# Evictions of the down result and transposes of the activations one place later in a mixture-of-experts stage

## The chip, the cores and the metric

The kernel runs on one core of a Trainium2 chip. The metric is the device time of one execution in microseconds (us). The core has a matmul engine (TensorE, PE in the profile; PEld are its weight loads), a vector engine (VectorE, DVE), a scalar engine (ScalarE, ACT), GpSimd (POOL, hardly used here) and SyncE (SP), which issues the transfers of the weights. Each engine runs its own list of instructions in order.

## The reference

Three transformer blocks on 256 tokens of width 1024 follow each other. The change is in the last step of the third, a mixture of 32 experts with four experts per token:

```python
def block_ffn(args):
    xb, e = args
    act = clamped_swiglu(xb @ w1[e] + b1[e])
    return act @ w2[e] + b2[e]
...
contrib = gate_sorted[:, None].astype(h.dtype) * y_buf[dest]
return jnp.zeros((T, D), h.dtype).at[sorted_tok].add(contrib)
```

A gate weighs each expert's result for each of its tokens, and the results are added. All inputs are float32.

## The kernel before

The method `moe` takes the experts in the order of their number of tokens, one per round `r`, 0 to 31. The first four (`BIGS`) have 128 rows for tokens, the others 64. A round has two parts. `up(r)` (L1840) multiplies the tokens of expert `r` with its up weights, 8 units of 1 MB each, 128x2048. `down(q, r)` (L1857) multiplies the activations of an earlier expert (from round 6 on `q = r - 2`) with its down weights, 4 units. So a round needs 12 MB.

A unit comes by a transfer into one of seven buffers (`raw` five times, `rawm`, `rawx`). Then `split` (L507) makes two halves of it: ACT writes the high half `whi` (L509), DVE subtracts it and writes the low half `wlo` (L510). There are three buffers for each half. PE multiplies with `whi`, then with `wlo`. For experts from 4 on, unit 1 of each part is not split; PE reads its raw buffer (`plain`), and the buffer is free when PE is through. All other buffers are free when DVE's subtraction is through.

All other work is put between the units by hand. `at(r, slot, f)` enters a step at one of 12 places of a round, and `run` calls the steps of a place: places 0 to 7 stand behind the first matmuls of the units of `up`, 8 to 11 in `down`. Each engine's list is exactly in this written order (`manual_schedule`). A step at place k stands on ACT and DVE behind the split of unit k and before that of unit k+1, and on PE between unit k's matmuls with `whi` and those with `wlo`.

The steps that matter here:

- `weigh(z, n)` (L1939), n = 0 and 1, evicts one half of the down result of expert `z = r - 3` from PSUM, times the gates: ACT writes `yh` (L1945), DVE writes `yl` (L1946). It waits for the down matmuls at the end of the round before.
- `activate(t)`, `silu(t)`, `gated(t)` work in even rounds on the up results of experts `r - 2` and `r - 1`, which share a tile: DVE clamps (L1878, L1879) at place 0, ACT takes silu (L1882) at place 1, DVE multiplies (L1886) at place 2.
- `turn(t)` (L1917) transposes these activations on PE, 8 matmuls of 128x128 into `atp` (L1923). `atp` and the down result `p2` share one PSUM buffer. Its `out(n)` (L1934, L1935) evicts them at places 6 and 7.
- `combine` (L1958) adds `yh` and `yl` of two experts to the output: matmuls `cbp` at places 4 to 7 of even rounds, an addition on DVE one place later.
- `take` and `fold` (L1898, L1911) at places 10 and 11 copy and add the up result. `gather` (`gp`, L1770, L1776) brings the tokens of four experts together, once per four rounds, in the down part of rounds 6, 10, ..., 26 and the up part of the odd rounds behind them.

After round 31 a tail works off experts 30 and 31; it doesn't use the places.

Of the kernel before, what the change touches and what calls it, by code (L numbers as in the profile page):

```python
# [434 lines left out]
class Net:  # L435
# [1202 lines left out]
    def moe(s, x, nm, ctx):  # L1638
# [114 lines left out]
        def gather(r, n):  # L1753


            G = mp.tile([128, 2, n, 128], F32R, name="G", tag="G", bufs=1)
            slots, w = ("iota", 128) if n == 2 else ("twice", SMALLS)
            for t in range(2):
                for a in range(n):
                    nc.vector.tensor_scalar(G[:, t, a], k_(slots), pos[:, t, r + a:r + a + 1], None,  # L1760
                                            op0=ALU.is_equal)
            xg = [mp.tile([128, 8, 2, 128], F32R, name="gx", tag="gx", bufs=3) for _ in range(2)]
            for a in range(n):
                X[r + a] = (xg[a][:, :, 0], xg[a][:, :, 1]) if n == 2 else xg[a // 2][:, :, a % 2]

            def chunk(k):
                p = aux("gp", (128, n, 2, w))
                for i, src in enumerate((hh, hl)):
                    for t in range(2):
                        mm(p[:, :, i], src[:, t, k * 128:(k + 1) * 128], G[:, t, :, 0:w], start=t == 0,  # L1770
                           stop=t == 1)

                def out():
                    for a in range(2):
                        q = p[:, a] if n == 2 else p[:, 2 * a:2 * a + 2].rearrange("p a b c -> p a (b c)")
                        nc.scalar.activation(xg[a][:, k], q, AF.Copy)  # L1776
                return out
            return [lambda k=k: chunk(k) for k in range(8)] + [lambda a=a: scatter(r + a, G[:, :, a])
                                                               for a in range(n)]
# [46 lines left out]
        def at(r, slot, *fs):  # L1826

            steps.setdefault((r + slot // 12, slot % 12), []).extend(fs)
# [5 lines left out]
        def pair_of(step, r, slot, behind=2):  # L1834

            at(r, slot, lambda: at(r, slot + behind, step()))
# [44 lines left out]
        def silu(r):  # L1881
            nc.scalar.activation(A[r][:, 0:1024], A[r][:, 0:1024], AF.Silu, scale=ALPHA)  # L1882

        def gated(r):
            b = A[r]
            nc.vector.scalar_tensor_tensor(b[:, 1024:2048], b[:, 1024:2048], 1.0, b[:, 0:1024], op0=ALU.add,  # L1886
                                           op1=ALU.mult)

        def take(r):

            p = P[r]
            if big(r) or r % 2 == 0:
                A[r] = mp.tile([128, 2048], F32, name="ml", tag="ml", bufs=1)
            if big(r):
                return bound(A[r], p[:, 0:1024], p[:, 1024:2048])
            own, other = halves(r)
            for ns in (slice(0, 1024), slice(1024, 2048)):
                nc.scalar.activation(A[r - r % 2][own, ns], p[other, ns], AF.Copy)  # L1898
# [5 lines left out]
        def fold(r, n):  # L1904

            if big(r):
                return
            own, _ = halves(r)
            ns = slice(n * 1024, n * 1024 + 1024)
            b = A[r - r % 2][own, ns]  # L1910
            nc.vector.tensor_add(b, b, P[r][own, ns])  # L1911

        def activate(r):
            if not big(r):
                bound(A[r], A[r][:, 0:1024], A[r][:, 1024:2048])

        def turn(r):  # L1917

            b = A[r]
            p = s.bank("atp", (128, 8, 128), "p2", 1)  # L1920
            t = mp.tile([128, 8, 2, 128], F32R, name="tp", tag="tp", bufs=1)
            for k in range(8):
                nc.tensor.transpose(p[:, k], b[:, 1024 + k * 128:1152 + k * 128], ident)  # L1923
            if big(r):
                hi, lo = A[r] = t[:, :, 0], t[:, :, 1]
            else:
                t5 = t.rearrange("p k a (b c) -> p k a b c", b=2)
                hi, lo = t5[:, :, :, 0], t5[:, :, :, 1]
                p = p.rearrange("p k (a c) -> p k a c", a=2)
                A[r], A[r + 1] = t[:, :, 0], t[:, :, 1]  # L1930

            def out(n):
                ks = slice(4 * n, 4 * n + 4)
                nc.scalar.activation(hi[:, ks], p[:, ks], AF.Copy, scale=1.0 / ALPHA)  # L1934
                nc.vector.scalar_tensor_tensor(lo[:, ks], p[:, ks], 1.0 / ALPHA, hi[:, ks].bitcast(F32),  # L1935
                                               op0=ALU.mult, op1=ALU.subtract)
            return out

        def weigh(r, n):  # L1939

            if n == 0:
                Y[r] = [mp.tile([128, 1024], F32R, name=a, tag=a, bufs=2) for a in ("yh", "yl")]
            yh, yl = Y[r]
            ns = slice(n * 512, n * 512 + 512)
            nc.scalar.activation(yh[:, ns], P[r][:, ns], AF.Copy, scale=GS[r])  # L1945
            nc.vector.scalar_tensor_tensor(yl[:, ns], P[r][:, ns], GS[r], yh[:, ns].bitcast(F32),  # L1946
                                           op0=ALU.mult, op1=ALU.subtract)
# [10 lines left out]
        def combine(r, c2):  # L1958

            p = aux("cbp", (128, 2, 256))  # L1960
            for c in range(2):
                back(p[:, c], 2 * c2 + c, (r, r + 1))
            o = acc[:, 2 * c2:2 * c2 + 2]
            return lambda: nc.vector.tensor_add(o, o, p)  # L1964
# [30 lines left out]
        for r in range(32):  # L1995
            q = r - 1 if r < BIGS else r - 2

            d = {0: (), 1: (), BIGS: (BIGS - 2,), BIGS + 1: (), BIGS + 2: (BIGS - 1,)}.get(
                r, (r - 2,) if r < BIGS else (r - 3,))
            for z in d:  # L2000
                at(r, 1, lambda z=z: weigh(z, 0))
                at(r, 2, lambda z=z: weigh(z, 1))
                if z % 2:
                    for c2 in range(4):
                        pair_of(lambda z=z, c2=c2: combine(z - 1, c2), r, 4 + c2, 1)
            t = r - 1 if r <= BIGS else r - 2 if r % 2 == 0 else -1
            if t >= 0:
                at(r, 0, lambda t=t: activate(t))
                at(r, 1, lambda t=t: silu(t))
                at(r, 2, lambda t=t: gated(t))  # L2010

                def turned(t=t, r=r):
                    out = turn(t)
                    at(r, 6, lambda: out(0))
                    at(r, 7, lambda: out(1))
                at(r, 3, turned)
            if r != 0:
                at(r, 9 if r == BIGS else 10, lambda r=r: take(r))
                at(r, 9 if r == BIGS else 10, lambda r=r: fold(r, 0))
                at(r, 9 if r == BIGS else 11, lambda r=r: fold(r, 1))  # L2020
            if r == 3 or r % 4 == 2 and BIGS < r < 30:
                g = r + 1 if r == 3 else r + 2
                spots = [(3, k) for k in range(12)] if r == 3 else (
                    [(r, 8 + k) for k in range(4)] + [(r + 1, k) for k in range(8)])

                def begin(g=g, spots=spots):
                    for f, (rr, k) in zip(gather(g, 4), spots):
                        if (rr, k) == spots[0]:
                            at(rr, k + 2, f())
                        else:  # L2030
                            pair_of(f, rr, k)
                at(*spots[0], begin)
# [238 lines left out]
```

## Time and profile before

| | |
|---|---|
| median of 3 runs | 2798.61 us (2796.19 to 2800.68) |
| the profiled execution | 2793.71 us, span 2791.9 us |
| busy in the span: PE, PEld | 2717.9 us (97%), 2364.8 us (85%) |
| busy in the span: DVE, ACT | 2245.2 us (80%), 1683.1 us (60%) |
| transfers over the span | 728.97 MB, 261 GB/s |
| transfers in fortieths 28 to 39 of the span | 384 to 413 GB/s |

The third block's experts fill the stretch from about 1680 us to the end. The span counts from the first instruction to the last; the time is the whole execution. In the timelines a row is one instruction, or several alike in a row (x8), with its start, its length, the names of what it writes and reads, and in brackets the idle time of the engine just before it and what ended that. `p` stands for the PSUM tiles of the up and the down product: `p<-whi,gx` is an up matmul, `p<-whi,tp` a down matmul.

### The profile page before, as it was taken

What the parts mean: (1) busy time and instruction counts of PE and PEld (TensorE: products, weight loads), DVE (VectorE), ACT (ScalarE), POOL (GpSimd) and SP (SyncE); (2) the same over time, 40 slices, a digit from 0 to 9 for tenths busy, and PEclk for the clock granted to TensorE, in tenths of its full rate; (3) what the DMA queues carried; (4) which work ended last, traced back from release to release, by engine and by line L of the source; (5) the groups of instructions that cost most, each with busy time, mean ns of one, the idle gap of its engine ahead of it and who ended that gap; (6) DMA issues with size and microseconds to landing.
All of it is one profiled execution on the core that took longest, in us unless ns stands there. A gap on an engine that the chain in (4) does not pass through costs nothing. (4 is left out here: it accounts for less than half of the span.)

```text
span 2791.9 us, 45884 instructions
## 1 busy us (share of the span) xinstructions
PE 2717.9 (97%) x17764; PEld 2364.8 (85%) x17764; DVE 2245.2 (80%) x3537; ACT 1683.1 (60%) x2658; POOL 3.3 (0%) x10
## 2 busy tenths in 40 slices
PE   9999999999999999999999998999999999999996
PEld 9999999999988999889999866877776767676764
DVE  7776777787776778888777754989999899999995
ACT  6554454464544545664467645777777777777773
POOL 0000000000000000000000000000000000000000
PEclk9999999999999999999999998999999999999998
DMA  7664466666653666437632333989999999999994
GB/s 290 229 227 166 173 221 240 244 224 242 227 182 122 236 243 225 150 139 256 234 142 96 111 118 120 359 306 384 395 405 395 398 402 389 405 387 400 388 413 161
DMA packets 102433, 728.97 MB, mean 261 GB/s; under 512 B 11384, under 2 KB 12920, under 8 KB 14528
## 3 DMA queue, kind: packets, MB, share of 16 engines
q1 hardware_dynamic: 99648, 719.64, 67.0%
q10 hardware_dynamic: 2560, 6.32, 0.7%
q8 instruction: 143, 2.34, 0.3%
q14 instruction: 82, 0.67, 0.1%
HBM read 723.80 MB, written 2.11 MB: 260 GB/s over the span
## 5 line engine op out<-in xcount | busy, mean ns | idle before, releaser
L510 DVE TENSOR_TENSOR wlo<-raw,whi 128x512 fp32r<-128x512 f32 (+1 forms) x1238 | 1178.7, 990 | 199.8 <-ACT whi L509 195.7
L509 ACT ACTIVATE whi<-raw 128x512 fp32r<-128x512 f32 (+1 forms) x1238 | 1006.6, 867 | 518.3 <-issue 283.1
L515 PE MATMUL gu<-xh,whi 128*128 128x256 f32 (+1 forms) x1760 | 499.7, 284 | 2.1 <-ACT whi L509 2.1
L517 PE MATMUL gu<-xh,wlo 128*128 128x256 f32 (+1 forms) x1760 | 497.6, 283 | 0.7 <-DVE wlo L510 0.7
L516 PE MATMUL gu<-xl,whi 128*128 128x256 f32 (+1 forms) x1760 | 498.1, 283 | 0.0
L515 PEld LDWEIGHTS gu<-xh,whi 128*128 128x128 f32 x1760 | 332.4, 189 | 2.9 <-ACT whi L509 2.5
L517 PEld LDWEIGHTS gu<-xh,wlo 128*128 128x128 f32 x1760 | 333.8, 190 | 1.1 <-DVE wlo L510 0.9
L516 PEld LDWEIGHTS gu<-xl,whi 128*128 128x128 f32 x1760 | 332.9, 189 | 0.3
L1848 PE MATMUL p<-whi,gx 128*128 128x512 f32 x1040 | 289.0, 404 | 2.5 <-ACT whi L509 2.5
L1848 PE MATMUL p<-wlo,gx 128*128 128x512 f32 x912 | 259.7, 407 | 23.6 <-DVE wlo L510 21.0
L517 PE MATMUL acc<-fh,wlo 128*128 128x256 f32 x880 | 245.5, 280 | 0.0
L516 PE MATMUL acc<-fl,whi 128*128 128x256 f32 x880 | 245.0, 280 | 0.1
L515 PE MATMUL acc<-fh,whi 128*128 128x256 f32 x880 | 242.4, 280 | 0.0
L1848 PEld LDWEIGHTS p<-whi,gx 128*128 128x128 f32 x1040 | 195.1, 189 | 54.5 <-issue 7.4
L1848 PEld LDWEIGHTS p<-wlo,gx 128*128 128x128 f32 x912 | 158.0, 189 | 78.7 <-DVE wlo L510 54.8
L516 PEld LDWEIGHTS acc<-fl,whi 128*128 128x128 f32 x880 | 165.8, 188 | 0.6 <-DVE fl L510 0.4
L517 PEld LDWEIGHTS acc<-fh,wlo 128*128 128x128 f32 x880 | 165.2, 188 | 0.0
L515 PEld LDWEIGHTS acc<-fh,whi 128*128 128x128 f32 x880 | 163.2, 187 | 1.2 <-ACT fh L509 0.8
L1870 PE MATMUL p<-whi,tp 128*128 128x512 f32 x464 | 154.0, 421 | 1.8 <-ACT whi L509 1.8
L1870 PE MATMUL p<-wlo,tp 128*128 128x512 f32 x400 | 128.8, 403 | 8.1 <-DVE wlo L510 8.1
L510 DVE TENSOR_TENSOR wlo<-rawm,whi 128x2048 fp32r<-128x2048 f32 x46 | 105.1, 2285 | 15.5 <-ACT whi L509 15.3
L1870 PEld LDWEIGHTS p<-whi,tp 128*128 128x128 f32 x464 | 87.1, 189 | 32.6 <-issue 11.5
(714 smaller groups left out, 5068.4 us busy)
## 6 DMA issues: line engine op xcount, KB each, us to landing
raw<-wmoe SPq DMA_DIRECT2D x276, 1024.0 KB, 7.9
raw<-wf SPq DMA_DIRECT2D x164, 1024.0 KB, 4.9
rawm<-wmoe SPq DMA_DIRECT2D x54, 1024.0 KB, 8.1
rawx<-wmoe SPq DMA_DIRECT2D x54, 1024.0 KB, 8.2
raw<-win SPq DMA_DIRECT2D x26, 1024.0 KB, 4.8
raw<-wada SPq DMA_DIRECT2D x24, 1024.0 KB, 4.8
raw<-wmod SPq DMA_DIRECT2D x24, 1024.0 KB, 5.1
raw<-wain SPq DMA_DIRECT2D x14, 1024.0 KB, 4.8
```

The costliest lines, as they stand in the source:

```text
L509: a = s.nc.scalar.activation(hi, x, AF.Copy)
L510: s.nc.vector.tensor_sub(lo, x, hi.bitcast(F32))
L515: mm(out, w[0], x[0], start=first, stop=False, skip_group_check=True)
L516: mm(out, w[0], x[1], start=False, stop=False, skip_group_check=True)
L517: mm(out, w[1], x[0], start=False, stop=last, skip_group_check=True)
L1848: mm(p[:, ns], xi, wi[:, ns], start=k == 0 and j == 0, stop=False, skip_group_check=True)
L1870: mm(p[:, n * 512:n * 512 + 512], xi, wi[:, c:c + 512], start=k == 0 and j == 0, stop=k == 7 and j == len(ts) - 1, skip_group_check=True)
```

## The change

Both halves of `weigh` stand one place later in the rounds, at 2 and 3 and not at 1 and 2. `turn` with its transposes stands at place 4 and not at 3. The evictions of the transposes stay at 6 and 7.

```diff
@@ -1998,8 +1998,8 @@
             for z in d:
-                at(r, 1, lambda z=z: weigh(z, 0))
-                at(r, 2, lambda z=z: weigh(z, 1))
+                at(r, 2, lambda z=z: weigh(z, 0))
+                at(r, 3, lambda z=z: weigh(z, 1))
                 if z % 2:
...
@@ -2013,7 +2013,7 @@
                     out = turn(t)
                     at(r, 6, lambda: out(0))
                     at(r, 7, lambda: out(1))
-                at(r, 3, turned)
+                at(r, 4, turned)
```

Round 12 on DVE, from the clamp on, as a piece of the difference (`p_23381` is the down result of expert 9):

```order
 L1878 TENSOR_SCALAR ml<-ml 128x1024
 L1879 TENSOR_SCALAR ml<-ml 128x1024
-L1946 SCALAR_TENSOR_TENSOR yl<-p_23381,gs,yh 128x512
 L510 TENSOR_TENSOR wlo<-raw,whi 128x2048
 L1946 SCALAR_TENSOR_TENSOR yl<-p_23381,gs,yh 128x512
 L1886 SCALAR_TENSOR_TENSOR ml<-ml 128x1024
-L510 TENSOR_TENSOR wlo<-raw,whi 128x2048 x2
+L510 TENSOR_TENSOR wlo<-raw,whi 128x2048
+L1946 SCALAR_TENSOR_TENSOR yl<-p_23381,gs,yh 128x512
+L510 TENSOR_TENSOR wlo<-raw,whi 128x2048
```

The eviction `yl` that stood ahead of the low half of unit 2 now stands behind that of unit 3; between units 2 and 3 there is one as before.

Round 12 on PE, the same way (`p_23438` is its up result; the first piece is unit 3 and the start of unit 4, the second the end of the first combine and what follows):

```order
@@ -12837,5 +12837,4 @@
 L1848 MATMUL p_23438<-wlo,gx 128x512 x4
 L1848 MATMUL p_23438<-whi,gx 128x512 x4
-L1923 MATMUL atp<-const,ml 128x128 x8
 L1848 MATMUL p_23438<-wlo,gx 128x512 x4
 L1848 MATMUL p_23438<-whi,gx 128x512 x4
@@ -12848,4 +12847,5 @@
 L1956 MATMUL cbp<-GT,yh 128x256
 L1956 MATMUL cbp<-GT,yl 128x256
+L1923 MATMUL atp<-const,ml 128x128 x8
 L1848 MATMUL p_23438<-wlo,gx 128x512 x4
 L1848 MATMUL p_23438<-whi,gx 128x512 x4
```

The eight transposes leave the place between the two products of unit 3 and stand between those of unit 4, behind the combine.

Round 13 on DVE, which has neither clamp nor transposes, from unit 0 on after the change (`p_23620` is the down result of expert 10):

```order
L510 TENSOR_TENSOR wlo<-rawm,whi 128x2048
L510 TENSOR_TENSOR wlo<-raw,whi 128x2048
L1946 SCALAR_TENSOR_TENSOR yl<-p_23620,gs,yh 128x512
L510 TENSOR_TENSOR wlo<-raw,whi 128x2048
L1946 SCALAR_TENSOR_TENSOR yl<-p_23620,gs,yh 128x512
L510 TENSOR_TENSOR wlo<-raw,whi 128x2048 x3
```

Before, the first `yl` stood right behind unit 0 and the second behind unit 2; now they stand behind units 2 and 3. On ACT `yh` moves in the same way.

## Rows read from the trace of the kernel before

**Rows 1.** Stretch: us, busy (x) of PE, PEld, DVE, ACT, POOL, PEclk, DMA share, GB/s.

```profile
2071.99:2102.01 30.02, 30.02 (x134) 22.30 (x133) 26.05 (x19) 25.09 (x28) 0.00 (x0) 1.00 1.00 405
2102.01:2135.72 33.71, 32.12 (x141) 23.25 (x140) 32.14 (x24) 23.47 (x17) 0.00 (x0) 1.00 0.94 374
2135.72:2163.45 27.73, 27.40 (x102) 18.39 (x101) 25.95 (x15) 21.55 (x14) 0.00 (x0) 1.00 1.01 423
1866.00:2723.00 857.00, 831.09 (x3538) 599.04 (x3537) 798.52 (x572) 645.68 (x541) 0.00 (x0) 1.00 0.98 397
```

**Rows 2.** Grouped waits, rounds 4 to 31: who for whom, us, times, longest.

```profile
ACT yh L1945 <- PE p L1870: 73.7, 26, 4.0
...
DVE wlo L510 <- ACT whi L509: 54.6, 53, 1.6
...
PE p L1848 <- DVE wlo L510: 20.8, 38, 1.0
```

**Rows 3.** Timeline of PE: round 6 (one row), round 12, round 30 (one row).

```profile
1920.58 1.20 PE L1848 MATMUL p<-wlo,gx 128*128 128x512 f32 x4 [1.01 <-DVE wlo L510]
...
2111.04 1.04 PE L1923 MATMUL atp<-const,ml 128*128 128x128 f32 x8
...
2113.07 1.20 PE L1848 MATMUL p<-wlo,gx 128*128 128x512 f32 x4 [0.99 <-DVE wlo L510]
...
2127.07 0.73 PE L1870 MATMUL p<-wlo,tp 128*128 128x512 f32 x2 [0.18 <-DVE wlo L510]
...
2128.57 3.60 PE L1870 MATMUL p<-raw,tp 128*128 128x512 f32 x8
...
2683.14 1.21 PE L1848 MATMUL p<-wlo,gx 128*128 128x512 f32 x4 [1.00 <-DVE wlo L510]
```

**Rows 4.** Timeline of ACT, round 12: start, length, instruction, [idle before <- releaser].

```profile
2102.21 0.69 ACT L1945 ACTIVATE yh<-p,gs 128x512 fp32r<-128x512 f32 x1 [3.11 <-PE p L1870]
2103.84 1.06 ACT L1882 ACTIVATE ml<-ml 128x1024 f32<-128x1024 f32 x1 [0.94 <-DVE ml L1878]
```

**Rows 5.** Timeline of DVE, round 12.

```profile
2104.44 0.75 DVE L1946 SCALAR_TENSOR_TENSOR yl<-p,gs,yh 128x512 fp32r<-128x512 f32 x1
2106.73 2.29 DVE L510 TENSOR_TENSOR wlo<-raw,whi 128x2048 fp32r<-128x2048 f32 x1 [1.54 <-ACT whi L509]
2108.94 0.75 DVE L1946 SCALAR_TENSOR_TENSOR yl<-p,gs,yh 128x512 fp32r<-128x512 f32 x1
2109.60 1.22 DVE L1886 SCALAR_TENSOR_TENSOR ml<-ml 128x1024 f32<-128x1024 f32 x1
```

**Rows 6.** Timeline of DVE, round 13.

```profile
2136.65 0.75 DVE L1946 SCALAR_TENSOR_TENSOR yl<-p,gs,yh 128x512 fp32r<-128x512 f32 x1 [0.18 <-ACT yh L1945]
...
2138.45 2.29 DVE L510 TENSOR_TENSOR wlo<-raw,whi 128x2048 fp32r<-128x2048 f32 x1 [1.05 <-ACT whi L509]
...
2154.53 2.28 DVE L510 TENSOR_TENSOR wlo<-raw,whi 128x2048 fp32r<-128x2048 f32 x1
```

**Rows 7.** Timeline of ACT, round 13.

```profile
2152.24 1.92 ACT L509 ACTIVATE whi<-raw 128x2048 fp32r<-128x2048 f32 x1 [2.24 <-DMA raw<-wmoe]
2154.64 1.93 ACT L1898 ACTIVATE ml<-p 64x1024 f32<-64x1024 f32 x2 [0.47 <-PE p L1854]
```

**Rows 8.** Busy time by stretch, end of round 12 and round 13.

```profile
2130.07:2133.24 3.17, 3.17 (x11) 1.77 (x10) 3.17 (x3) 1.93 (x2) 0.00 (x0) 1.00 0.61 215
...
2136.41:2152.24 15.83, 15.59 (x58) 10.17 (x56) 14.61 (x9) 13.51 (x9) 0.00 (x0) 1.00 1.01 424
```

**Rows 9.** Timeline of ACT, round 17.

```profile
2280.33 1.92 ACT L509 ACTIVATE whi<-raw 128x2048 fp32r<-128x2048 f32 x1 [3.05 <-DMA raw<-wmoe]
```

**Rows 10.** Timeline of DVE, round 11.

```profile
2074.80 2.29 DVE L510 TENSOR_TENSOR wlo<-raw,whi 128x2048 fp32r<-128x2048 f32 x1 [1.60 <-ACT whi L509]
```

**Rows 11.** Busy time by stretch, behind round 31.

```profile
2738.00:2744.00 6.00, 5.99 (x38) 5.95 (x39) 2.13 (x4) 0.71 (x2) 0.00 (x0) 0.72 0.56 233
```

**Rows 12.** Timeline of PE, behind round 31.

```profile
2738.01 1.15 PE L1923 MATMUL atp<-const,ml 128*128 128x128 f32 x8 [4.34 <-DVE ml L1886]
```

## The prediction

> **What bounds the kernel now.** I read four views in this order: busy time by stretch, the grouped waits, the timeline of single rounds, and the transfers.
>
> The first has a row each for rounds 11, 12 and 13, and one for rounds 4 to 31. It shows that the change lives in a stage where three resources are nearly full. Over the 857 us of the last row PE is busy 831.09 us, DVE 798.52 us (93%), and the transfers run at 397 GB/s, while the stretch of round 13 alone shows 423 GB/s, which I take as the ceiling [rows 1]. 423 against 397 is 6% of slack for the transfers; DVE has 7%. So a delay in one engine is soon one of the others, and a hole that is filled need not shorten anything. The single rounds differ: round 13 runs at 423 GB/s and is full of transfers, round 12 moves 374 GB/s and has PE idle 33.71 - 32.12 = 1.59 us, round 11 has PE busy without a gap.
>
> The waits show what the change aims at and what it may touch. ACT stands 73.7 us in 26 waits in front of the first eviction (yh) until the down matmuls end, though later splits could run [rows 2]. DVE stands 54.6 us before splits whose high half ACT has not made. PE stands only 20.8 us for low halves, and that small number is the one that costs directly.
>
> Where PE stands, the timeline tells: in each of the thirteen even rounds 6 to 30 it waits 0.99 to 1.01 us for the low half of unit 3, right behind the transposes; the first, one of the middle and the last are shown [rows 3]. So even rounds go at DVE's pace at that point, and the eight transposes (1.04 us in the row) lie ahead of that wait: they are now free, they fill a hole that would otherwise be 2 us long.
>
> **The change part by part, an even round (round 12).** DVE's chain to that wait is: clamp, then ACT's silu, ACT's high half of unit 2, DVE's low half of unit 2, one yl, gated, low half of unit 3. ACT waits for yh until 2102.21 but then stands again for the clamp until 2103.84 [rows 4]. Taking yh out ahead of silu therefore frees nothing: silu still waits for the clamp, unit 2 is still split at the same time. DVE waits 1.54 us for it at 2106.73, and its first yl (0.75 us at 2104.44) lies ahead of that wait, in time that is idle anyway [rows 5].
>
> After the change this yl stands behind the low half of unit 2, where the second stood; the second stands behind unit 3. The low half of unit 3 starts at the same time as before, but one yl is now added to the full part of DVE's round behind it. One costs 0.75 us by its row, or 2109.60 - 2108.94 = 0.66 us by starts [rows 5]. I take 0.70. DVE's idle time ahead of unit 2 grows by the same.
>
> On PE the transposes go behind unit 4's first matmuls and the first combine. The wait for unit 3 grows from 0.99 to about 2.0 us, and their 1.04 us (less, since a pipelined tail is counted) now comes on top. What of this survives to the end of the round is decided at the first down unit, where PE already waits 0.18 us for DVE at 2127.07 [rows 3]: PE comes at most 1.04 - 0.18 = 0.86 us late, DVE 0.66 to 0.75. Both ways the round ends later by about 0.70 us, and 13 x 0.70 = **+9.1 us**. Bounds: 0.66 to 0.86 each, 8.6 to 11.2.
>
> **An odd round without gather (round 13; also 9, 17, 21, 25, 29, 31).** Here nothing stands between yh and the split of unit 2, so ACT can split while the down matmuls still run. DVE loses 0.18 and 1.05 us at present [rows 6], and both go: it can take 1.23 us back. It is late by 0.70 when it comes, so it would be 0.5 us early at the round's end. But that has a floor. Down unit 2 is split only when its load has landed: ACT waits 2.24 us for that until 2152.24, then splits 1.92 us, to 2154.16, and DVE takes it at 2154.53 [rows 6, 7]. This load is late because the transfers pause at 2130 to 2133 (215 GB/s) and are full at 424 GB/s from there to the landing [rows 8]. The pause ends where PE ends the plain down unit, 2128.57 + 3.60 = 2132.17 [rows 3], whose buffer the next load in the queue takes; PE comes there 0.70 us late. So the load lands at 2152.94, ACT ends its split at 2154.86, its copies of the up result start there and not at 2154.64, and all behind them is 0.22 to 0.33 us late. Of 0.70, about 0.43 is taken back. In round 17 the same wait is 3.05 us long [rows 9], so there less is. Bounds: nothing, and the whole 1.23. I take 0.43, since the load's row decides, for six rounds (behind 31 comes the tail): **-2.6 us**.
>
> **An odd round with gather (7, 11, ..., 27).** DVE waits 1.60 us there [rows 10], but PE has no gap in the whole round (30.02 of 30.02 busy, [rows 1]): what DVE gains, nobody waits for, and what PE brings along stays. Price zero; upper bound of a gain 6 x 1.60 = 9.6 us.
>
> **Rounds 1 to 4 and the rest.** Transposes move in these four as well, and weights of experts 0 to 2. Three products per unit keep PE behind no split there; I price it at nothing, with 4 x 0.70 = 2.8 us to either side. No transfer, no instruction and no buffer is added; SP and POOL keep their order. The transposes still come before place 6, where their eviction stands; ACT then waits up to 2 us for them, and has that time, as the second eviction waits for DVE anyway. What is late next is the first down unit on DVE.
>
> **Sum.** 9.1 - 2.6 = +6.5 us. The profiled execution took 2793.7 us, so 2800.2 by it. That execution is 4.9 us below the median shown; on the median's scale the forecast is 2798.6 + 6.5 = **2805.1 us**. About 0.2% (5.6 us) can be told from no change here.
>
> **The rivals.**
>
> *Faster: DVE alone sets the pace.* For it: DVE is 93% busy, its idle time is nearly all waits for ACT, and the change is made for these. Against it: rounds 11 and 13 are full on PE and on transfers. If it were so, the odd rounds would give 7 x 1.23 + 6 x 1.60 = 18.2 us and the even ones cost 13 x 0.75 = 9.75: -8.5, or 2790.1 us. The Trainium skill (Perfetto Trace Analysis, Identifying the Most-Contended Engine) speaks for this rival: matmul busy time says little, judge TensorE by its weight loads, the vector engine by its occupancy. By it PE stands at 599.04 of 857 us (70%) and DVE is the one to relieve; this case's 1.00 us waits on PE agree with that in even rounds only. Chance 0.17.
>
> *No change: the odd rounds give it all back.* Should the load land in time, because low halves of units 2 and 3 end 1.1 us earlier and their buffers with them, six rounds return 1.23 each: 9.1 - 7.4 = +1.7, or 2800.3 us. For it: the transfers' mean is still 6% below the ceiling. Against it: the queue is full just there. Chance 0.23. Here also falls the case that PE takes nothing from the move.
>
> *Clearly slower: PE's clock falls in the longer hole.* Before, waits of 1.0 us go with a granted clock of 1.00, 2.4 GHz [rows 1]; behind the 4.34 us that PE stands near the end it is 0.72 in the mean of 6 us, a mix of 1.2 and 2.4 GHz [rows 11, 12], which costs 0.28 x 6 = 1.7 us. A hole of 2.0 us lies between, nearer the first. If it decided in all thirteen: +22 on top of 6.5, 2827 us; if the loads came later still in the odd rounds with gather, some 10 us over the forecast. Together 0.08. The Trainium skill (TensorE: Matmul & The Clock Gate, Part 1) has the clock go by how busy the engine was of late and halves it after idling; by that rule alone the change would be punished in each even round, and no row before shows a hole of this length.
>
> **How the numbers follow.** Forecast 0.52, whose own range is +3 to +11 (2802 to 2810); some 0.14 of it falls below 5.6 us. Slower by over 0.2%: 0.38 + 0.08 = 0.46. Within 0.2%: 0.23 + 0.14 = 0.37. Faster: 0.17. The range 2791 to 2813 takes in the bounds of the even rounds (+11.2 and 2.8 for the first rounds), the case of no change and the near edge of the faster rival, and leaves out most of that rival and the clock.
>
> **What would show it.** Right: PE's wait for unit 3 in even rounds about 1.9 instead of 1.0 us, transposes behind it; DVE's wait ahead of unit 2 in even rounds 2.2 instead of 1.54; in rounds like 13 ACT's wait for yh short, DVE's 1.05 us gone, but down unit 2 still waiting for its load; four rounds together 0.9 to 1.0 us longer than now. Wrong: even rounds of unchanged length, or the load of round 13 landing without a wait and the round shorter by over a microsecond (no change or faster); a clock below 1.00 in even rounds (clock); DVE's waits much shorter with PE's unit 3 wait back near 1 us (faster).

## The result: slower by 0.7%, outside the range, and the profile after

The change takes 2816.96 us (median of 7 runs, 2812.36 to 2826.37), before 2798.61 us; the ratio is 1.0071, with a 95% interval of 1.0051 to 1.0092. The forecast was 2805.1 us, within 2791 to 2813: the direction was right, the size was not.

The page of the changed kernel, its span and the busy time of the engines:

```profile
span 2824.6 us, 45919 instructions
...
PE 2735.2 (97%) x17764; PEld 2384.2 (84%) x17764; DVE 2244.7 (79%) x3537; ACT 1686.4 (60%) x2658; POOL 3.3 (0%) x10
```

The profiled execution is one of the longer ones, 2826.4 us. Part of that is no matter of the change: the experts' stage begins at 1692.3 us here and at 1677.6 us before, and all code ahead of it is the same. The granted clock in the 80 us ahead of the stage is 0.79 here (first row below) and 1.00 before; an experiment below had 0.81, and a second profile of the changed kernel 1.00. So I compare inside the stage.

Busy time by stretch, changed kernel, columns as in [rows 1]: ahead of the stage, rounds 4 to 31, and 6 us from just ahead of the low half of unit 3 in round 10 and in round 12:

```profile
1612.00:1692.00 80.00, 78.21 (x368) 52.08 (x366) 36.20 (x97) 28.39 (x75) 0.00 (x0) 0.79 0.28 94
...
1881.00:2756.00 875.00, 833.79 (x3542) 610.48 (x3541) 798.15 (x573) 649.02 (x540) 0.00 (x0) 0.99 0.96 388
...
2065.50:2071.50 6.00, 5.67 (x26) 5.06 (x27) 6.00 (x6) 3.21 (x3) 0.00 (x0) 0.72 1.02 422
2133.20:2139.20 6.00, 5.66 (x33) 4.99 (x34) 6.00 (x6) 4.76 (x4) 0.00 (x0) 1.00 1.01 412
```

Rounds 4 to 31 take 875 us in place of 857 [rows 1], with the same busy time of DVE and 2.7 us more of PE, and 388 GB/s in place of 397. The last two rows are the find: they start at the same place of the program and show PE busy for the same time, but in one it comes through 26 matmuls and in the other through 33, at a granted clock of 0.72 and of 1.00.

Grouped waits, changed kernel, 1881 to 2756 us:

```profile
DVE wlo L510 <- ACT whi L509: 73.9, 57, 3.0
ACT ml L1882 <- DVE ml L1878: 60.4, 13, 4.7
...
PE p L1848 <- DVE wlo L510: 38.2, 42, 2.0
...
ACT yh L1945 <- DVE yl L1946: 16.3, 20, 1.0
```

Of ACT's 73.7 us in front of yh behind the down matmuls [rows 2], 2.9 us are left. In their place ACT stands 60.4 us in front of silu, its next instruction in even rounds (12.4 us before), and 16.3 us in front of yh for DVE. DVE's waits for ACT grew from 54.6 to 73.9 us, PE's for DVE from 20.8 to 38.2 us. Most of the wait that the change removes comes back as two others.

PE in rounds 10 and 12, changed kernel, answering to [rows 3]: unit 3's low half, then the first combine (in round 10) and the transposes:

```profile
2065.84 1.20 PE L1848 MATMUL p<-wlo,gx 128*128 128x512 f32 x4 [2.01 <-DVE wlo L510]
2066.87 1.79 PE L1848 MATMUL p<-whi,gx 128*128 128x512 f32 x4
2068.46 0.41 PE L1956 MATMUL cbp<-GT,yh 128*128 128x256 f32 x1
...
2070.17 1.16 PE L1923 MATMUL atp<-const,ml 128*128 128x128 f32 x8
...
2133.54 1.19 PE L1848 MATMUL p<-wlo,gx 128*128 128x512 f32 x4 [1.99 <-DVE wlo L510]
...
2136.45 1.03 PE L1923 MATMUL atp<-const,ml 128*128 128x128 f32 x8
```

The hole is 1.99 to 2.01 us in all thirteen even rounds, as forecast. From its end to the transposes PE needs 2136.45 - 2133.54 = 2.91 us in round 12 and 2070.17 - 2065.84 = 4.33 us in round 10, for the same instructions: the clock fell to its lower level, 1.2 GHz, and a combine matmul takes 0.41 in place of 0.28 us. It fell so in seven of thirteen: rounds 6, 10, 14, 16, 20, 22, 26.

DVE in rounds 12 and 13, changed kernel, answering to [rows 5, 6]:

```profile
2127.08 2.29 DVE L510 TENSOR_TENSOR wlo<-raw,whi 128x2048 fp32r<-128x2048 f32 x1 [2.33 <-ACT whi L509]
2129.40 0.75 DVE L1946 SCALAR_TENSOR_TENSOR yl<-p,gs,yh 128x512 fp32r<-128x512 f32 x1
...
2131.20 2.29 DVE L510 TENSOR_TENSOR wlo<-raw,whi 128x2048 fp32r<-128x2048 f32 x1
2133.41 0.75 DVE L1946 SCALAR_TENSOR_TENSOR yl<-p,gs,yh 128x512 fp32r<-128x512 f32 x1
2134.07 2.28 DVE L510 TENSOR_TENSOR wlo<-raw,whi 128x2048 fp32r<-128x2048 f32 x1
2136.26 2.29 DVE L510 TENSOR_TENSOR wlo<-rawm,whi 128x2048 fp32r<-128x2048 f32 x1
...
2157.53 2.28 DVE L510 TENSOR_TENSOR wlo<-raw,whi 128x2048 fp32r<-128x2048 f32 x1
2159.73 0.73 DVE L1946 SCALAR_TENSOR_TENSOR yl<-p,gs,yh 128x512 fp32r<-128x512 f32 x1
...
2176.49 2.29 DVE L510 TENSOR_TENSOR wlo<-raw,whi 128x2048 fp32r<-128x2048 f32 x1 [2.15 <-ACT whi L509]
```

ACT in rounds 12 and 13, changed kernel, answering to [rows 4, 7]:

```profile
2124.19 1.06 ACT L1882 ACTIVATE ml<-ml 128x1024 f32<-128x1024 f32 x1 [4.74 <-DVE ml L1878]
...
2157.06 0.69 ACT L1945 ACTIVATE yh<-p,gs 128x512 fp32r<-128x512 f32 x1 [0.41 <-PE p L1870]
...
2174.54 1.91 ACT L509 ACTIVATE whi<-raw 128x2048 fp32r<-128x2048 f32 x1 [3.86 <-DMA raw<-wmoe]
```

In round 12 DVE waits 2.33 us ahead of unit 2 (1.54 before), as silu stands 4.74 us for the clamp; the second yl now lies between the low halves of units 3 and 4. In round 13 both of DVE's early waits are gone, but then it stands 2.15 us for down unit 2, whose load lands late.

### The profile page after: what moved, and what is told of

Its sections match the earlier page's. It is cut to its first block, busy times and chain, and to the rows that moved or that the text cites. A ratio compares the mean times of both kernels' runs of the same rounds, so it can differ in the third digit from the quotient of the medians.

```text
span 2824.6 us, 45919 instructions
## 1 busy us (share of the span) xinstructions
PE 2735.2 (97%) x17764; PEld 2384.2 (84%) x17764; DVE 2244.7 (79%) x3537; ACT 1686.4 (60%) x2658; POOL 3.3 (0%) x10
## 5 line engine op out<-in xcount | busy, mean ns | idle before, releaser
L1848 PE MATMUL p<-whi,gx 128*128 128x512 f32 x1040 | 295.3, 411 | 2.5 <-ACT whi L509 2.5
```

What stands on the lines that cost most here:

```text
L1848: mm(p[:, ns], xi, wi[:, ns], start=k == 0 and j == 0, stop=False, skip_group_check=True)
```

## The experiments

One measure serves for all kernels: the time on PE from the low half of unit 3 in round 6 to that in round 30, twelve steps of two rounds. Each step holds one odd round; where that is one with gather (7, 11, ..., 27) I call it a gather step, else (9, 13, ..., 29) a plain step. A fall is a hole behind which the granted clock over 6 us is 0.72. Each row is from one profile, the ratio from the runs.

| kernel | round 6 to 30, us | against before | hole, us | falls of 13 | ratio to before, 95% |
|---|---|---|---|---|---|
| before | 762.56 | | 1.00 | 0 | |
| the change | 780.94 | +18.4 | 2.0 | 7 | 1.0071 (1.0051 to 1.0092) |
| the change, second profile | 781.28 | +18.7 | 2.0 | 8 | 1.0053 (1.0030 to 1.0076) |
| even rounds only | 780.80 | +18.2 | 2.0 | 6 | 1.0063 (1.0034 to 1.0091) |
| odd rounds only | 765.13 | +2.6 | 1.00 | 0 | 1.0005 (0.9985 to 1.0025) |
| transposes only | 775.05 | +12.5 | 1.88 | 5 | 1.0040 (1.0017 to 1.0062) |
| change, hole filled | 772.49 | +9.9 | 1.12 | 0 | 1.0038 (1.0018 to 1.0058) |
| change, half filled | 773.78 | +11.2 | 1.57 | 0 | 1.0056 (1.0031 to 1.0081) |
| before, fewer loads | 761.05 | -1.5 | 1.00 | 0 | 1.0006 (0.9988 to 1.0023) |
| the same, odd rounds changed | 752.59 | -10.0 | 1.00 | 0 | 0.9952 (0.9933 to 0.9971) |
| silu earlier | 747.78 | -14.8 | none | 0 | 0.9933 (0.9907 to 0.9958) |
| silu earlier and the change | 748.88 | -13.7 | none | 0 | 0.9952 (0.9933 to 0.9971) |

**The hole filled.** Eight idle transposes of a constant stand where the change took the real ones away, so PE has work ahead of unit 3 and all else is as in the change.

```diff
+        def fill():
+            p = aux("idle", (128, 4, 128))
+            for k in range(8):
+                nc.tensor.transpose(p[:, k % 4], ident, ident)
...
+                at(r, 3, fill)
                 at(r, 4, turned)
```

> The change, with eight transposes of a constant put on PE at place 3, where the moved ones stood; nothing reads them. They are PE work that the hole ahead of unit 3 hides. Theory A (clock): the hole shrinks from 2.0 to 1.0 us, the granted clock is 1.00 in all thirteen even rounds, and the seven falls with some 1.3 us each are gone: the expert stage falls from 1132.3 us to about 1123, and what is left over before (1114.3) is about 8 us, 0.7 a round. Theory B (order): the evictions' place on DVE is what costs; the clock falls in time that would be waited away. Then the stage stays at 1130 to 1133 us.

PE in round 10 of this kernel, the filling and the wait behind it:

```profile
2052.34 1.04 PE L1996 MATMUL idle<-const 128*128 128x128 f32 x8
2054.50 1.19 PE L1848 MATMUL p<-wlo,gx 128*128 128x512 f32 x4 [1.12 <-DVE wlo L510]
```

No fall in thirteen rounds, and +9.9 us in place of +18.4: what the order of the work costs without the clock. Its stage came to 1128.7 us, between the two theories (3.4 us of what it has over before lie ahead of round 6, where idle transposes stand too; among kernels that leave that stretch alone it differs by up to 1.8 us). Both hold a part each. The clock's part is best read inside one kernel: in the change a gather step without a fall (round 18 to 20) is 0.77 us longer than before, the five with a fall 2.03 to 2.05. A fall costs 2.04 - 0.77 = 1.27 us, and seven cost 8.9.

**The transposes alone.** The evictions stay, `turn` goes to place 4.

```diff
-                at(r, 3, turned)
+                at(r, 4, turned)
```

> The transposes alone at place 4; the evictions stand at 1 and 2 as before. Theory A: PE's hole is 2.0 us here too, the clock falls in about half of the even rounds, and the stage takes 1114 + 7 x 1.3 + up to 13 x 0.7, 1123 to 1132 us. Theory B: without a further eviction in the full part of DVE's round the first down unit is on time, so 1114 to 1117 us.

PE in round 12, then busy time by stretch in rounds 12 and 10:

```profile
2122.84 1.43 PE L1848 MATMUL p<-wlo,gx 128*128 128x512 f32 x4 [1.88 <-DVE wlo L510]
2124.06 1.91 PE L1848 MATMUL p<-whi,gx 128*128 128x512 f32 x4
```

```profile
2122.50:2128.50 6.00, 5.66 (x26) 5.00 (x27) 5.68 (x5) 2.04 (x2) 0.00 (x0) 0.72 1.01 414
2056.50:2062.50 6.00, 5.68 (x33) 5.01 (x34) 6.00 (x5) 3.63 (x3) 0.00 (x0) 1.00 1.01 418
```

The hole of 1.88 us makes the clock fall without the evictions' move, in rounds 12, 16, 20, 24, 28 here. Steps ahead of the first fall are 0.37 to 0.40 us longer than before, so of the 0.77 us the transposes are about half, the evictions the other. All five falls lie in plain steps, which are 1.9 to 2.0 us longer than before, so a fall costs 1.5 to 1.6 us there. The stage came to 1132.4 us, just above theory A's range, with 3.5 us of it over before ahead of round 6.

**Even and odd rounds apart.** Two kernels; in the first the odd rounds keep the old places of `weigh`, in the second only they get the new ones (and the transposes stay).

```diff
+                late = 0 if r % 2 and r > BIGS else 1
+                at(r, 1 + late, lambda z=z: weigh(z, 0))
+                at(r, 2 + late, lambda z=z: weigh(z, 1))
...
-                at(r, 3, turned)
+                at(r, 4, turned)
```

```diff
+                late = r % 2 if r > BIGS else 0
+                at(r, 1 + late, lambda z=z: weigh(z, 0))
+                at(r, 2 + late, lambda z=z: weigh(z, 1))
```

> Evictions and transposes later in the even rounds (and 1 to 4) alone; odd rounds as before. By the prediction the odd rounds without gather then give nothing back and the stage is 2 to 3 us longer than with the whole change, about 1135 us, with the same 2.0 us holes and falls of the clock. If the odd rounds' share of the change were a loss and not a return, it is shorter than 1132 us.

> The evictions one place later in the odd rounds from 7 on alone; even rounds and transposes as before. No hole in PE's work grows. By the prediction's step for odd rounds the load of down unit 2 sets the floor, and each of the seven rounds without gather gives back about 0.4 us: stage 1111 to 1112 us. If nothing holds it, 7 x 1.23 = 8.6 us: 1106 us. If the transfers' queue decides alone: 1114 us, no change.

The even rounds carry the whole loss, +18.2 us. I had expected this kernel's stage to be 2 to 3 us longer than the change's; it is 2.2 us longer (1134.5 against 1132.3), but that difference lies behind round 30 and is no sign of a return in the odd rounds. In the second kernel they give nothing back: its stage is 1119.3 us, above all three values that I had put (1.8 us of it over before lie ahead of round 6), and its steps are within 0.1 us of before but for two (+0.54 between rounds 12 and 14, +2.04 between 28 and 30). Where the gain goes is seen behind round 9 of the second kernel. ACT, DVE and PE, a row each:

```profile
2041.34 1.92 ACT L509 ACTIVATE whi<-raw 128x2048 fp32r<-128x2048 f32 x1 [3.07 <-DMA raw<-wmoe]
```

```profile
2043.29 2.29 DVE L510 TENSOR_TENSOR wlo<-raw,whi 128x2048 fp32r<-128x2048 f32 x1 [1.44 <-ACT whi L509]
```

```profile
2053.10 1.21 PE L1848 MATMUL p<-wlo,gx 128*128 128x512 f32 x4 [1.00 <-DVE wlo L510]
```

DVE comes early to down unit 2, then stands 1.44 us, since ACT has waited 3.07 us for the load (2.52 in that round before), and PE gets a new wait of 1.00 us at unit 0 of round 10.

**Fewer loads.** To see whether loads are that floor, unit 1 of the down part of the 64-row experts is multiplied with a tile that lies in the chip already; these weights are left out of the result, and a round has 11 loads. Once with the order of before, once with the odd rounds changed as above.

```diff
+            if not big(r) and k == 1 and what == "down":
+                return True, (hh.rearrange("p a b -> p (a b)").bitcast(F32),)
```

> The kernel before, in which the plain unit 1 of the down part of the 64-row experts is multiplied with a tile that is already in the chip instead of loaded weights: 11 of 12 loads of a round are left, and this part of the weights is left out of the result. Only the base for the next kernel. Stage shorter than 1114 us by 5 to 40 us, as one transfer in twelve (2.5 us at 423 GB/s) goes from 28 rounds; the odd rounds' waits for loads should be gone.

> The same lighter kernel with the evictions of the down result one place later in the odd rounds alone (the same weights left out). If late loads were the reason that the odd rounds gave nothing back (my step (b)), this is now faster than the lighter kernel before by 0.4 to 1.2 us in each of six or seven odd rounds, 3 to 8 us between the first and the last even round. If PE itself or DVE's sum of work sets the odd rounds, the difference is within 2 us, as it was with all loads (+2.6, of which 2.0 in one place).

Round 13 on DVE, first the lighter kernel before, then the lighter kernel with odd rounds changed:

```profile
2137.77 0.75 DVE L1948 SCALAR_TENSOR_TENSOR yl<-p,gs,yh 128x512 fp32r<-128x512 f32 x1 [0.18 <-ACT yh L1947]
2139.57 2.29 DVE L510 TENSOR_TENSOR wlo<-raw,whi 128x2048 fp32r<-128x2048 f32 x1 [1.05 <-ACT whi L509]
...
2155.65 2.28 DVE L510 TENSOR_TENSOR wlo<-raw,whi 128x2048 fp32r<-128x2048 f32 x1
```

```profile
2140.97 2.27 DVE L510 TENSOR_TENSOR wlo<-raw,whi 128x2048 fp32r<-128x2048 f32 x1
2143.18 0.73 DVE L1948 SCALAR_TENSOR_TENSOR yl<-p,gs,yh 128x512 fp32r<-128x512 f32 x1
...
2157.71 2.27 DVE L510 TENSOR_TENSOR wlo<-raw,whi 128x2048 fp32r<-128x2048 f32 x1
```

Taking a twelfth of the loads away is worth 1.5 us (2.4 us of the stage, where I had 5 as the least): the waits for loads shrink, ACT's in round 13 from 2.24 to 0.36 us, but DVE's 0.18 and 1.05 us stand as before, and the round is as long. With the odd rounds changed both of these go, and now the six plain steps are 1.36 to 1.43 us shorter than in the lighter kernel before, -8.5 us in all, a little more than the 3 to 8 that I had put; gather steps are unchanged within 0.05 us. So the gain in rounds like 13 is there to be had, and with all loads it is lost to the load, or to the buffer that this waits for: the lighter kernel takes away both at once and doesn't tell these two apart.

**Silu earlier.** The chain to the hole is clamp, silu, split of unit 2. Here the clamp of the gates stands at place 11 of the round before, and silu at place 0, in front of the split of unit 1; once on the kernel before, once on the change.

```diff
-                at(r, 1, lambda t=t: silu(t))
+                at(r, 1 if big(t) else 0, lambda t=t: silu(t))
...
+            if r > BIGS and r % 2 and r < 31:
+                at(r, 11, lambda r=r: clamp(r - 1))
```

> The kernel before with only this: in rounds of 64-row experts the clamp of the gates (the first of the two clamps) stands at place 11 of the round before and silu at place 0 of the even round, so ACT no longer has to wait for the clamp before it can split unit 2. Theory A (the hole ahead of unit 3 comes from the chain clamp, silu, high half of unit 2): DVE's wait of about 1.5 us ahead of unit 2 in even rounds goes, PE's hole ahead of unit 3 falls from 1.0 to under 0.4 us, the thirteen even rounds win up to 0.7 us each; the expert stage comes to 1105 to 1111 us (before 1114.3), the time about 2790 to 2796 against 2799. Theory C (transfers alone set the length of two rounds together): the hole goes but the stage stays within 2 us of 1114.

> The change with the same move of clamp and silu. If the loss of the change stands wholly on the 2.0 us holes ahead of unit 3 in even rounds and on the clock that falls in them (theory A), holes fall to about 1.3 us or less, the clock falls in none or one of thirteen, and of the 18 us that the change costs between the first and last even round over 8 us come back: stage 1118 to 1125 us. If the order of DVE's work alone costs (theory B), the stage stays at 1128 to 1133 us with or without falls.

Round 12 of the first of them, on DVE (unit 2 behind the first yl), then on PE (transposes and the low half of unit 3):

```profile
2108.18 0.75 DVE L1953 SCALAR_TENSOR_TENSOR yl<-p,gs,yh 128x512 fp32r<-128x512 f32 x1
2108.84 2.29 DVE L510 TENSOR_TENSOR wlo<-raw,whi 128x2048 fp32r<-128x2048 f32 x1
```

```profile
2114.83 1.04 PE L1930 MATMUL atp<-const,ml 128*128 128x128 f32 x8
2115.62 1.17 PE L1848 MATMUL p<-wlo,gx 128*128 128x512 f32 x4
```

Busy time by stretch of the same kernel, round 13 and rounds 4 to 31:

```profile
2136.90:2165.00 28.10, 27.74 (x103) 18.73 (x102) 25.53 (x14) 21.62 (x14) 0.00 (x0) 1.00 1.01 422
1875.00:2722.00 847.00, 828.14 (x3555) 603.45 (x3555) 803.52 (x574) 652.31 (x543) 0.00 (x0) 1.00 0.99 404
```

DVE's 1.54 us and PE's hole are gone. This kernel takes 2778.35 us against 2798.41, a ratio of 0.9933 (0.9907 to 0.9958): it beats both. I had expected at most 0.7 us a round, by PE's hole; it is 1.60 to 1.63 us in each gather step, DVE's whole wait and a little. Plain steps win 0.3 to 1.5 us; their odd rounds run at the transfers' ceiling, 422 GB/s in round 13 [rows 1, 8]. The stage came to 1100.0 us, below the 1105 to 1111 expected. On top of this move the change costs 1.1 us (748.88 against 747.78), not 18.4: theory A as put there asked for 8 us back, and all but one came. The stage with both is 1099.0 us, far under the 1118 to 1125 expected: that sum counted what comes back of the change's loss, and not that the move shortens the kernel before as well. With no wait behind the clamp there is no hole for the transposes to fill, and no idle time of DVE that the first yl could use up.

The Trainium skill (Perfetto Trace Analysis, Optimization Strategy) says to look for the gaps of the engine one has found to be contended, and to make what they wait for start sooner. These runs agree: the gap was DVE's 1.54 us, what it waited for was silu, and moving that was worth 14.8 us.

**Half the filling, and the change once more.** To see where the fall begins, four idle transposes in place of eight; and a second profile of the change.

```diff
-            for k in range(8):
+            for k in range(4):
```

> The change with four idle transposes, not eight, ahead of PE's wait for the low half of unit 3: the hole should be about 1.55 us, between the 1.12 us with eight and the 2.0 us with none. If the clock falls by the length of the hole with a sharp bound, none or all of thirteen fall; if it falls now and then, two to four do, and between the first and the last even round the kernel loses 10 us (order alone) plus about 1.4 us for each fall.

> The change itself once more, for a second profile: holes of 2.0 us again in all thirteen even rounds. If the rounds in which the clock falls are fixed by the program, the same seven fall (6, 10, 14, 16, 20, 22, 26); if not, another set of about five to eight. The loss between the first and the last even round should be 10 us plus about 1.3 us for each fall.

Half filled, PE in round 10 and busy time by stretch in rounds 10 and 12:

```profile
2051.86 1.21 PE L1848 MATMUL p<-wlo,gx 128*128 128x512 f32 x4 [1.56 <-DVE wlo L510]
```

```profile
2051.60:2057.60 6.00, 5.74 (x33) 5.03 (x34) 6.00 (x6) 4.76 (x4) 0.00 (x0) 1.00 1.01 419
2118.00:2124.00 6.00, 5.70 (x33) 5.01 (x34) 6.00 (x6) 4.78 (x4) 0.00 (x0) 1.00 1.01 412
```

No fall at 1.57 us, and +11.2 us. In the second profile of the change the same seven rounds fall again, and round 30 too (that fall lies behind the end of the measure); the other five stay at 1.00 again. The hole is as long in the others, so its length alone doesn't set a falling round apart.

The traces tell more of it. In the change, the granted clock of 1 us just ahead of the fall in round 6, then just behind the falls in rounds 6, 10 and 14:

```profile
1936.28:1937.28 1.00, 0.99 (x4) 0.86 (x5) 1.00 (x2) 1.00 (x2) 0.00 (x0) 1.00 0.97 410
1937.30:1938.30 1.00, 1.00 (x4) 0.78 (x3) 1.00 (x1) 1.00 (x1) 0.00 (x0) 0.50 1.09 410
2067.00:2068.00 1.00, 1.00 (x4) 0.74 (x3) 1.00 (x1) 1.00 (x1) 0.00 (x0) 0.50 1.07 442
2196.71:2197.71 1.00, 1.00 (x4) 0.73 (x3) 1.00 (x2) 1.00 (x2) 0.00 (x0) 0.50 1.05 434
```

The falls begin at 1937.29, 2067.00 and 2196.70 us, each when PE has been at work again for 0.5 to 1.2 us (0.2 to 1.6 us over all 26 falls of four profiles). Wherever two rounds four apart both fell, 16 pairs, the falls are 129.71 us apart, though the holes ahead of them begin 129.2 to 130.5 us apart. So the falls keep a time of their own, and what goes with falling is where a hole lies against it, not the round. In the two profiles of the change the holes lay nearly alike (in round 6 the fall came 3.01 and 3.17 us behind the hole's start), so the same seven rounds don't show that the program fixes them.

## Why the prediction was wrong

**The step that failed is the price of the clock.** The forecast was told with PE's clock at nothing, because a hole of 2.0 us "lies between, nearer the first" of two rows, one of 1.0 us with a clock of 1.00 and one of 4.34 us with 0.72; the case had its share in a chance of 0.08. The runs show seven or eight falls of 1.27 us, 9 to 10 us, about half of the loss. The rival's own price was sound (0.28 x 6 = 1.7 us; measured 1.42 us from the hole to the transposes, 1.27 in the whole step), its count (thirteen) too high. An interpolation between two rows said nothing on a quantity that jumps between two levels. The Trainium skill (TensorE: Matmul & The Clock Gate, Part 1), by which idling throttles the clock, deserved more weight than I gave it. These runs agree as to the direction: none of 13 rounds fell at holes of 1.00, 1.12 and 1.57 us each, five at 1.88, six to eight at 2.0. But no rule by the length of the hole alone fits them, neither "none" nor "in each even round", since equal holes fell in some rounds and not in others.

**Even rounds, +0.70 each: right in kind, a little small.** Silu waits for the clamp, unit 2 comes no earlier, the hole is 2.0 us. The step without a fall is +0.77: of DVE's starts in round 12, the low half of unit 3 to that of unit 4 is 2134.07 - 2131.20 = 2.87 us, with a yl between, and from there to the next, with nothing between, 2136.26 - 2134.07 = 2.19, so the yl adds 0.68; and the low half of unit 2 to the yl behind it is 2.32 us now, 2.21 before [rows 5], 0.11 more. Thirteen make 10.0, not 9.1.

**Odd rounds without gather, -2.6: failed.** The mechanism stood: DVE's waits go, and down unit 2's load is the floor. But round 13 doesn't stand for all six. A round can give back only as much as DVE comes late to down unit 2, counted from the end of ACT's split of it. Before, that is 0.37 us in round 13, but 0.03 in rounds 17 and 21, 0.08 in 9, 0.31 in 25, 0.56 in 29. And "the load lands at 2152.94", so many us behind the end of the plain down unit on PE as before, was wrong for round 13 itself. Before, from the end of the plain unit at 2132.17 [rows 3] to the landing at 2152.24 are 20.07 us. After, PE's plain unit of round 12 ends at 2153.30 and the load is there at 2174.54, 21.24 us, 1.17 later than my rule has it; in the other five rounds the rule holds within 0.33 us. With 0.77 for the even round and 1.27 for a fall taken off, round 13 is 0.7 us longer, rounds 25 and 29 give back 0.3 each, and the other three are within 0.2 us of nothing. Even the bound of "nothing" was not low enough, since odd rounds alone came to +2.6, by rounds 13 and 29.

What round 13 meets is seen in the transfers from the end of the plain unit to the landing, by queue (packets, MB, share of the 16 engines), after (2153.3 to 2174.0 us) and before (2132.2 to 2151.7 us):

```profile
q1 hardware_dynamic: 1098, 8.06, 94.9%
q8 instruction: 1, 0.02, 0.3%
```

```profile
q1 hardware_dynamic: 1036, 7.54, 94.1%
```

After the change a transfer of instructions falls into the stretch: 16 KB in one packet, from 2171.20 on, 1.07 us long, where an 8 KB packet of a load takes 0.31. The load closes with sixteen packets of 4 bytes; fifteen start by 2172.72, the last at 2173.98. Before, that transfer began at 2151.91, when the load was through. In eight profiles of kernels with all loads, the stretch up to ACT's start is 21.07 to 21.86 us in the 23 of these odd rounds that held such a transfer in full, and 19.88 to 20.66 in 22 of the 25 others. That it holds up one engine, and with it the load, fits these times but is not shown by an experiment; and it doesn't explain the other three, the longest of them (22.57) in round 29 with the odd rounds alone changed. Without the load the rounds give 1.4 us, a little above my upper bound of 1.23.

**Odd rounds with gather, zero: right**, within 0.05 us with the odd rounds changed alone and with fewer loads. **Rounds 1 to 4, zero within 2.8: right**, from the stage's start to round 6 it takes 244.0 and 243.7 us in the two profiles of the change, 243.0 before.

**The sum again**: 10.0 for the even rounds, 0 for the odd ones, 7 x 1.27 = 8.9 for the clock, 18.9 us; 18.35 between the medians. The medians alone would not show the clock's share: the intervals of the half filled kernel and of the change overlap widely. It rests on the profiles, where steps with and without a fall stand side by side.

**The rivals.** DVE alone as the bound was right for even rounds, but there the change adds to DVE's idle time and takes nothing from it. No change (the odd rounds return 1.23 each) needed a load in time, and it was not. Clearly slower was the one that came, at two thirds of its size.

## What to carry to other kernels

When a step leaves the place ahead of a wait, ask what the wait hangs on: what stood there was free, and the wait stays. Removing the largest wait of a list (73.7 us) moved it by one instruction; the one worth removing, 12.4 us in the same list, was the one at whose end DVE and then PE stood waiting, silu behind the clamp. And a longer hole on PE is to be priced with the clock's lower level as a whole case, not between two levels.

## What was unexpected of the hardware

The granted clock fell behind some holes of 2.0 us and of 1.88 us and not behind others of the same length; at 1.57 us and below it never fell. Falls four rounds apart came 129.71 us apart each time, though the holes ahead of them did not. A transfer of instructions, 16 KB among loads of 1 MB, goes with a load that lands about 1 us later. And a kernel that loads a twelfth less was no faster (1.0006), though the transfers of rounds like 13 had run at their ceiling: DVE's two early waits and the landing of the load were limits of nearly equal height, and taking one away shows only the other.
